# The low part of the queries times the high half of the keys only, with the two maps in the two row halves of the array

## The chip, the core and the metric

The kernel runs on one core of a Trainium2 chip. The core has a matrix engine (TensorE, PE in the rows, with its weight loads as PEld), a vector engine (VectorE, DVE), an activation engine (ScalarE, ACT), a general engine (GpSimd, POOL), and a queue for transfers on SyncE (SP). The metric is the device time of one execution in microseconds (us). Lower is better.

## What is computed

One layer of a backbone with two parallel branches: differential attention and a bidirectional state-space scan. Only the attention over the 2048 latent tokens is touched by the change. Each of 8 heads has two score maps of width 64 and one value of width 128. The keys are the 2048 latent ones and 256 cached ones, 2304 in all.

```python
s = jnp.einsum('bqhcd,bkhcd->bchqk', qi, k).astype(F32) * scale
p = jax.nn.softmax(s, axis=-1)
a = p[:, 0] - lam * p[:, 1]
return jnp.einsum('bhqk,bkhd->bqhd', a.astype(v.dtype), v)
```

Here c is the map (0 or 1). Everything is in float32.

## The kernel before

TensorE takes float32 operands in a fast form (float32r) that rounds them. So the kernel splits every operand into a high part and a low part and adds products of the parts. It runs in three stages: projections and scan (to about 1550 us), attention over the latent tokens (about 1550 to 2790), and the output projection (to the end).

**A unit of attention** is one head and 128 query rows. There are 8 x 16 = 128 units. `frame(i)` writes out the work of four units at different depths: the scores of unit i, the exponentials of unit i-1 (`s_exp`) and its combination of the two maps (`combine`), the transposes of unit i-2 (`t_high`, `t_low`), and the products with the values of the units before that (`av`).

- **Scores.** `s_chunk(i, k)` makes one chunk: map m = k // 3 against 768 keys (j = k % 3). A key tile K (128 x 768) holds the high half of one map's keys in rows 0 to 63 and the low half in rows 64 to 127. The query tile q holds the same part of the queries in both row halves: index l = 0 is the high part, l = 1 the low part. So two matmuls on all 128 rows give (high q) x (high k + low k) and (low q) x (high k + low k). Each is done for two times 384 keys: four matmuls a chunk, 24 a unit. All four write one PSUM tile `ps_s`. The pool `psS` has two of them, for both maps together.
- **Eviction.** One VectorE instruction a chunk copies `ps_s` to the score rows S0 or S1 and takes the row maximum. `s_max` reduces the three maxima of a map to one.
- **Exponentials.** ScalarE makes one exp over 2304 elements for each map, with the row sum (`s_exp`). VectorE turns the two sums into a factor `sm` (reciprocal, then one small instruction), and GpSimd adds the two maps with it (`combine`).
- **Transposes.** Three transposes on TensorE fill one `ps_t`. ScalarE casts it to aH (`t_high`), then VectorE subtracts aH and writes aL (`t_low`): six times a unit.
- **Values.** 54 matmuls into `ps_o` for each pair of units, from aH, aL and V.

**What sets the order.** The code does not issue instructions. It records them in a `Plan`, which gives each a price (`price`) and a due time, plays the program through with these prices, and emits each engine's instructions in the order that comes out. That order is fixed when the kernel is built. Each engine then works strictly in its order, and waits where an operand or a buffer isn't ready.

Every instruction is emitted from one line of the recorder (L232 in the rows), so rows are told apart by the names of the tiles.

Of the kernel before, what the change touches and what calls it, by code (L numbers as in the profile page):

```python
# [9 lines left out]
F32 = mybir.dt.float32  # L10
# [3 lines left out]
ALU = mybir.AluOpType  # L14
# [4 lines left out]
P = 128  # L19
# [7 lines left out]
NKEY = LAT + PAST  # L27
NH = 8
# [166 lines left out]
class Plan:  # L195


    def __init__(self, tc):
        self.tc, self.ops, self.last, self.floor, self.line = tc, [], None, None, None
        for k in ("tensor", "vector", "scalar", "gpsimd", "sync"):  # L200
            setattr(self, k, Engine(self, k))

# [12 lines left out]
    def add(self, eng, name, args, kw):  # L215
        i = len(self.ops)
        if name == "dma_start":
            q, eng = eng, "dma"
        named = dict(kw)
        for k, v in enumerate(args):  # L220
            named["out" if k == 0 else f"arg{k}"] = v
        writes, reads = [], []
        for k, v in named.items():
            if isinstance(v, View):
                (writes if k in ("out", "accum_out") else reads).append(v)
        if name == "matmul" and not kw["start"]:
            reads.append(named["out"])

        def emit():
            rl = lambda v: v.real() if isinstance(v, View) else v  # L230
            e = getattr(self.tc.nc, q if name == "dma_start" else eng)
            getattr(e, name)(*[rl(v) for v in args], **{k: rl(v) for k, v in kw.items()})  # L232

        op = Op(i, eng, emit, self.price(eng, name, named))
        f = str(named.get("func", "")).rsplit(".", 1)[-1]
        op.tab = TABLE.get(f)
        inside = sum(isinstance(v, View) and not v.t.pool.psum and math.prod(v.shape[1:]) > 1
                     for k, v in named.items() if k not in ("out", "accum_out"))
        twice = name in ("tensor_scalar", "tensor_copy") and inside
        op.port = eng == "gpsimd" or eng == "vector" and (inside > 1 or twice)  # L240
        if self.floor is not None:
            op.deps.add(self.floor)
        if self.line is not None and eng == "dma":
            op.weak.update(self.line)
            self.line[:] = [i]
        self.ops.append(op)
        for v in reads + writes:
            s = v.t
            if not s.users:
                op.deps.add(s.pool.op)  # L250
                if s.prev is not None:
                    op.weak.add(s.prev.users[0])
                if s.old is not None:
                    op.deps.update(s.old.users)
                    s.old.dead = True
            else:
                op.weak.add(s.users[0])
            if s.dead:
                raise RuntimeError(f"{s.kw} is used after its slot went to another")
        for v in reads:  # L260
            self.touch(op, v, False)
        for v in writes:
            self.touch(op, v, True)
        op.deps.discard(i)
        op.weak.discard(i)
        op.weak -= op.deps

    def touch(self, op, v, write):
        s = v.t
# [19 lines left out]
    def price(self, eng, name, a):  # L289
        size = lambda v: math.prod(v.shape[1:])  # L290
        o = a.get("out")
        ins = [v for k, v in a.items() if k != "out" and hasattr(v, "shape")]
        if eng == "dma":
            named_in = a["in_"]
            run = min(4096, 4 * min(o.shape[-1], named_in.shape[-1]))
            return max(math.prod(o.shape) * 4 / run * max(9.7 + 0.0365 * run, 28.4) / 16, 180.0) if run > 4 else 180.0
        n = max([size(o)] + [size(v) for v in ins[:1]])
        if eng == "tensor":
            if name == "transpose":
                return 108.0  # L300
            fast = a["lhsT"].t.args[1] == F32R
            m = size(o)
            k = 1.0 if fast else 4.0
            if not fast and a["rhs"].shape[-1] <= 2:
                return 213.0
            return max(m / 2.4 + 13.3, 109.0) if fast else max(m * k / 2.4 + 13.3, 213.0)
        psum = any(isinstance(v, View) and v.t.pool.psum for v in ins)
        if eng == "scalar":
            extra = sum(1 for k in ("bias", "scale") if isinstance(a.get(k), View)) * 93
            return n * 0.833 * 1.0 + (52 if psum else 94) + extra + (93 if "accum_out" in a else 0)  # L310
        if eng == "gpsimd":
            if name == "tensor_tensor":
                thin = any(st[0] == "unsqueeze" and st[1] == (2,) for st in a["in1"].steps)
                return n * (1.66 if thin else 2.1) + 150
            if name == "memset":
                return 36.0
            if name == "tensor_copy":
                return 127.0
            if name == "affine_select":
                return 594.0  # L320
            return n * 0.84 + 240
        if name == "reciprocal":
            return n * 6.25 + 70
        extra = 60 * sum(1 for k in ("scalar", "scalar1", "scalar2") if isinstance(a.get(k), View))
        if name == "tensor_scalar" and not psum:
            return n * 0.53 + 10 + max(extra, 60)
        if name in ("tensor_reduce", "reduce_sum", "reduce_max"):
            return n * (1.042 if ins[0].plain else 1.72) + 70
        return n * 1.042 + 66 + extra
# [113 lines left out]
def body(tc, I, O):  # L443
    pl = Plan(tc)
    nc = pl
    es = ExitStack()
    mm = nc.tensor.matmul
# [254 lines left out]
    for g, wm in enumerate(wms):  # L702
# [4 lines left out]
        if g in (2, 5):  # L707
            for j in range(2):
                acc = vp.tile([P, 384], F32, tag=f"ga{j}", name="macc")[:, :n]
                nc.vector.tensor_scalar(out=acc, in0=wm[:, 0, :n], scalar1=cond[:, j * 8:j * 8 + 1], scalar2=None,  # L710
                                        op0=ALU.mult)
# [8 lines left out]
        ps = bank("y")  # L720
# [4 lines left out]
        for f in range(n // P):  # L725
# [8 lines left out]
                                   op0=ALU.add, op1=ALU.mult)  # L734
# [604 lines left out]
    def load_k(h, m, j):  # L1339
        t = kpool.tile([P, 768], F32R, tag="K", name="K", bufs=9)  # L1340
        for r, src in enumerate((kH_d, kL_d)):
            load(out=t[r * 64:r * 64 + 64].bitcast(F32),
                 in_=src[h, m * 64:m * 64 + 64, SEQ + j * 768:SEQ + (j + 1) * 768])
        Kt[h, m, j] = t
# [127 lines left out]
            u.sm = u.pool.tile([P, 4], F32, tag="sm", name="sm", bufs=2)  # L1472
        return U[i]

    def s_chunk(i, k):
        u = get_unit(i)
        m, j = k // NG, k % NG
        if j == 0:
            u.S[m] = u.pool.tile([P, NKEY], F32, tag=f"S{m}", name=f"S{m}", bufs=2)
        ps = psS.tile([P, 2, 512], F32, tag="S", name="ps_s")  # L1480
        kt = Kt[u.h, m, j]
        for l in range(2):
            for a in range(2):
                mm(ps[:, a, :384], lhsT=u.pr.q[:, l, m, u.qo:u.qo + P], rhs=kt[:, a * 384:(a + 1) * 384],
                   start=l == 0, stop=l == 1)
        src, dst = ps[:, :, :384], u.S[m][:, j * 768:(j + 1) * 768]
        nc.vector.tensor_scalar(out=dst.rearrange("p (a b) -> p a b", a=2), in0=src, scalar1=1.0, scalar2=None,
                                op0=ALU.mult, op1=ALU.max, accum_out=u.mx[:, m, j:j + 1])

    def s_max(i):  # L1490
        u = U[i]
# [91 lines left out]
    def frame(i):  # L1583
        live = i < NU
        if live:
            get_unit(i)
            if i % 2 == 1 and i + 1 < NU:
                get_pair((i + 1) // 2)
        ti = i - 2
        tl = 0 <= ti < NU  # L1590
        if 0 <= i - 1 < NU:
            s_exp(i - 1, 0)
            s_exp(i - 1, 1)
            combine(i - 1)
        j = i - 16
        for k in range(6):
            if live:
                s_chunk(i, k)
                h, r = i // 16, i % 16
                if r == 15 and h + 1 < NH and k >= 3:  # L1600
                    load_k(h + 1, 1, k - 3)
                if r == 5 and h + 1 < NH and k < 3:
                    load_k(h + 1, 0, k)
                if r == 6 and h + 1 < NH and k < 2:
                    load_v(h + 1, k, 0)
            if tl:
                t_high(ti, k)
                t_low(ti, k)
            if k % 2 == 0:
                av((i - 3) * 3 + k // 2 - 1)  # L1610
        if live:
            s_max(i)
        if j >= 0 and j // 16 + 1 < NH:
            if j % 16 == 2:
                load_v(j // 16 + 1, 0, 1)
                load_v(j // 16 + 1, 1, 1)
            if j % 16 == 3:
                load_v(j // 16 + 1, 0, 2)
                load_v(j // 16 + 1, 1, 2)
        U.pop(i - 3, None)  # L1620
# [221 lines left out]
```

## Time and profile before

| what | value |
|---|---|
| median of 3 runs | 3195.61 us (3192.19 to 3200.39) |
| the profiled execution | 3202.35 us, its span 3200.6 us |
| TensorE busy, whole span | 3136.2 us (98%) |
| VectorE, ScalarE, GpSimd busy, whole span | 2321.5, 1907.6, 1302.4 us |
| granted TensorE clock, mean | 0.994 of full speed |

The span reaches from the first to the last instruction; 1.75 us of the profiled time lie around it. Busy shares are means over stages with different limits, so the attention stage has to be read by itself. The ends of matmuls are modelled, so the distance between the starts of neighbouring matmuls tells more than the duration of one.

### The profile page before, as it was taken

The page shows a single profiled execution, that of the slowest core. Times are in us where ns is not written, and L with a number is a line of the kernel's source. Part 1 is how long each engine was busy: PE and PEld are TensorE (multiplying, and loading weights), DVE is VectorE, ACT ScalarE, POOL GpSimd, SP SyncE. Part 2 cuts the span into 40 slices and gives each one's busy share as a digit, 9 for nine tenths or more (in the row PEclk, how much of TensorE's full clock was granted, in tenths as well). Part 3 has the DMA queues.
Part 4 walks back from the last instruction along what each step waited for, and adds up shares of the span by engine and source line. Part 5 has one row for each costly group of instructions (what it writes and reads, how often), then busy time and mean ns, then how long its engine had stood idle before and what let it go on. Part 6 is the DMA issues. An engine that isn't in the chain of part 4 may idle for free. (4 is left out here: it accounts for less than half of the span.)

```text
span 3200.6 us, 55106 instructions
## 1 busy us (share of the span) xinstructions
PE 3136.2 (98%) x19875; PEld 2932.6 (92%) x19875; DVE 2321.5 (73%) x4701; ACT 1907.6 (60%) x3461; POOL 1302.4 (41%) x1120
## 2 busy tenths in 40 slices
PE   8999999999999999999999999999999999999999
PEld 5999999988899999998999999999999999977877
DVE  5544524766665776654599999999999999977775
ACT  4233322333466677663578878888888788864442
POOL 1011000000021122120399999999999999900000
PEclk9999999999999999999999999999999999999999
DMA  8632422867678777878413131313222211296663
GB/s 282 216 113 98 134 81 93 252 185 224 201 224 248 210 212 211 216 188 210 114 34 95 34 97 37 93 40 89 59 75 64 64 51 54 76 282 191 176 189 102
DMA packets 490722, 449.21 MB, mean 140 GB/s; under 512 B 34991, under 2 KB 437704, under 8 KB 490450
## 3 DMA queue, kind: packets, MB, share of 16 engines
q1 hardware_dynamic: 488530, 445.52, 47.6%
q8 instruction: 158, 2.59, 0.3%
q14 instruction: 114, 0.93, 0.1%
q10 hardware_dynamic: 1920, 0.17, 0.0%
HBM read 305.96 MB, written 139.62 MB: 139 GB/s over the span
## 5 line engine op out<-in xcount | busy, mean ns | idle before, releaser
L232 DVE TENSOR_SCALAR_CACHE_REDUCE S<-ps_s 128x768 f32<-128x768 f32 x768 | 716.8, 951 | 17.3 <-PE ps_s L232 11.3
L232 POOL TENSOR_TENSOR S<-S,S 128x768 f32<-128x768 f32 x384 | 710.0, 1866 | 10.1
L232 PE MATMUL ps_p<-hH,wH 128*128 128x384 f32 (+1 forms) x2112 | 698.6, 331 | 0.0
L232 PE MATMUL ps_p<-hL,wH 128*128 128x384 f32 (+1 forms) x2112 | 692.3, 328 | 0.0
L232 PE MATMUL ps_p<-hH,wL 128*128 128x384 f32 (+1 forms) x2112 | 690.9, 327 | 0.0
L232 PE MATMUL ps_s<-K,q 128*128 128x384 f32 x3072 | 678.1, 345 | 0.2
L232 ACT ACTIVATE S<-S,mx 128x2304 f32<-128x2304 f32 x256 | 569.2, 2224 | 82.3 <-DVE mx L232 82.2
L232 PEld LDWEIGHTS ps_s<-K,q 128*128 128x128 f32 x3072 | 504.5, 189 | 3.4 <-DVE S L232 1.1
L232 PE MATMUL ps_o<-aH,V 128*128 128x256 f32 x2304 | 506.4, 295 | 0.1
L232 POOL TENSOR_SCALAR_AFFINE_SELECT ar<-ar 128x512 f32<-128x512 f32 x136 | 115.7, 857 | 786.4 <-ACT ea L232 646.8
L232 DVE TENSOR_TENSOR aL<-ps_t,aH 128x384 fp32r<-128x384 f32 x768 | 406.5, 552 | 40.2 <-ACT aH L232 31.7
L232 ACT CAST aH<-ps_t 128x384 fp32r<-128x384 f32 x768 | 344.3, 478 | 122.2 <-PE ps_t L232 120.7
L232 PEld LDWEIGHTS ps_p<-hL,wH 128*128 128x128 f32 x2112 | 399.3, 189 | 1.7 <-issue 1.4
L232 PEld LDWEIGHTS ps_p<-hH,wH 128*128 128x128 f32 x2112 | 399.4, 189 | 0.9 <-issue 0.5
L232 PEld LDWEIGHTS ps_p<-hH,wL 128*128 128x128 f32 x2112 | 398.8, 189 | 1.3 <-issue 1.2
L232 POOL TENSOR_SCALAR S<-S,sm 128x768 f32<-128x768 f32 x384 | 349.3, 919 | 99.7 <-DVE sm L232 45.5
L232 PEld LDWEIGHTS ps_o<-aH,V 128*128 128x128 f32 x2304 | 382.0, 189 | 0.7 <-ACT aH L232 0.5
L232 PE MATMUL ps_t<-cst,S 128*128 128x128 f32 x2304 | 380.1, 275 | 0.2
L232 PEld LDWEIGHTS ps_t<-cst,S 128*128 128x128 f32 x2304 | 285.4, 140 | 50.4 <-POOL S L232 16.2
L232 PE MATMUL ps_o<-aL,V 128*128 128x256 f32 x1152 | 330.0, 286 | 0.0
L232 DVE TENSOR_TENSOR wL<-wr,wH 128x1024 fp32r<-128x1024 f32 x88 | 108.7, 1235 | 199.6 <-ACT wH L232 196.9
L232 PEld LDWEIGHTS ps_o<-aL,V 128*128 128x128 f32 x1152 | 218.8, 190 | 0.1
(245 smaller groups left out, 4882.1 us busy)
## 6 DMA issues: line engine op xcount, KB each, us to landing
wr<-in_w_in SPq DMA_DIRECT2D x88, 512.0 KB
ar<-row_d SPq DMA_DIRECT2D x68, 512.0 KB
q<-qH_d SPq DMA_DIRECT2D x128, 128.0 KB
q<-qL_d SPq DMA_DIRECT2D x128, 128.0 KB
xb<-xbc_d SPq DMA_DIRECT2D x17, 640.0 KB
K<-kH_d SPq DMA_DIRECT2D x48, 192.0 KB
K<-kL_d SPq DMA_DIRECT2D x48, 192.0 KB
V<-vH_d SPq DMA_DIRECT2D x24, 384.0 KB
```

Of the source, the lines that this page charges most:

```text
L232: getattr(e, name)(*[rl(v) for v in args], **{k: rl(v) for k, v in kw.items()})
```

## The change

The scores of a unit are now made in three pairs (`s_pair`): for the same 768 keys both maps at once, each in its own `ps_s`. The high part of the queries still multiplies both halves of the keys, on all 128 rows. The low part multiplies the high half of the keys only: the product of the two low parts is left out of the sum. That matmul needs 64 rows. The key tile of map 1 is loaded with its halves exchanged (`r ^ m`), so that the high half lies in rows 0 to 63 for map 0 and in rows 64 to 127 for map 1. The four low matmuls of a pair alternate between the two row halves of the array, and `together` makes them one entry of the plan, so that nothing comes between them. The price of a matmul on 64 rows is set anew. The loads of the next head's map 1 are recorded after each pair of a head's last unit, not after the chunks 3 to 5.

```diff
@@ add
+        if self.one:
+            op = self.ops[self.one[0]]
+            op.emit = lambda a=op.emit: (a(), emit())
+            op.cost += self.price(eng, name, named)
+            i = op.i
...
+    def together(self, f):
+
+        self.one = []
+        f()
+        self.one = None
...
@@ price
+            if fast and a["lhsT"].shape[0] == 64:
+                return max(m / 4.8 + 13.3, 109.0)
...
@@ load_k
         for r, src in enumerate((kH_d, kL_d)):
+            r = r ^ m
...
-    def s_chunk(i, k):
+    def s_pair(i, j):
+
         u = get_unit(i)
-        m, j = k // NG, k % NG
         if j == 0:
-            u.S[m] = u.pool.tile([P, NKEY], F32, tag=f"S{m}", name=f"S{m}", bufs=2)
-        ps = psS.tile([P, 2, 512], F32, tag="S", name="ps_s")
-        kt = Kt[u.h, m, j]
-        for l in range(2):
+            for m in range(2):
+                u.S[m] = u.pool.tile([P, NKEY], F32, tag=f"S{m}", name=f"S{m}", bufs=2)
+        ps = [psS.tile([P, 2, 512], F32, tag="S", name="ps_s") for m in range(2)]
+        for m in range(2):
             for a in range(2):
-                mm(ps[:, a, :384], lhsT=u.pr.q[:, l, m, u.qo:u.qo + P], rhs=kt[:, a * 384:(a + 1) * 384],
-                   start=l == 0, stop=l == 1)
...
+                mm(ps[m][:, a, :384], lhsT=u.pr.q[:, 0, m, u.qo:u.qo + P], rhs=Kt[u.h, m, j][:, a * 384:(a + 1) * 384],
+                   start=True, stop=False)
+
+        def low():
+            for a in range(2):
+                for m in range(2):
+                    r = slice(m * 64, m * 64 + 64)
+                    mm(ps[m][:, a, :384], lhsT=u.pr.q[r, 1, m, u.qo:u.qo + P],
+                       rhs=Kt[u.h, m, j][r, a * 384:(a + 1) * 384], start=False, stop=True)
+        pl.together(low)
+        for m in range(2):
+            nc.vector.tensor_scalar(out=u.S[m][:, j * 768:(j + 1) * 768].rearrange("p (a b) -> p a b", a=2),
+                                    in0=ps[m][:, :, :384], scalar1=1.0, scalar2=None,
+                                    op0=ALU.mult, op1=ALU.max, accum_out=u.mx[:, m, j:j + 1])
...
@@ frame
-                s_chunk(i, k)
                 h, r = i // 16, i % 16
-                if r == 15 and h + 1 < NH and k >= 3:
-                    load_k(h + 1, 1, k - 3)
+                if k % 2 == 0:
+                    s_pair(i, k // 2)
+                    if r == 15 and h + 1 < NH:
+                        load_k(h + 1, 1, k // 2)
```

**The order on TensorE, one pair.** These rows of the program before stand in the middle of the attention stage; `ps_s_22446` and `ps_s_22463` are two chunks of the same map, one after the other in the two buffers.

```order
L232 MATMUL ps_s_22446<-K_19977,q_22143 128x384 x4
L232 MATMUL ps_t_22455<-cst_83,S0_22168 128x128 x3
L232 MATMUL ps_s_22463<-K_20048,q_22143 128x384 x4
L232 MATMUL ps_t_22470<-cst_83,S0_22168 128x128 x3
L232 MATMUL ps_o_22339<-aH_22260,V_20261 128x256
```

After the change, one pair is `ps_s_22195` (map 0) and `ps_s_22206` (map 1), the second pair of its unit.

```order
L232 MATMUL ps_s_22195<-K_20050,q_21841 128x384 x2
L232 MATMUL ps_o_22067<-aH_21971,V_20293 128x256
L232 MATMUL ps_o_22067<-aH_21971,V_20286 128x256
L232 MATMUL ps_o_22067<-aL_21983,V_20286 128x256
L232 MATMUL ps_t_22203<-cst_83,S0_21899 128x128
L232 MATMUL ps_s_22206<-K_22071,q_21841 128x384 x2
L232 MATMUL ps_s_22195<-K_20050,q_21841 128x384
L232 MATMUL ps_s_22206<-K_22071,q_21841 128x384
L232 MATMUL ps_s_22195<-K_20050,q_21841 128x384
L232 MATMUL ps_s_22206<-K_22071,q_21841 128x384
L232 MATMUL ps_t_22203<-cst_83,S0_21899 128x128 x2
```

A tile was complete after four matmuls in a row; now both tiles are open until the last of the four low matmuls, and the next pair needs both buffers back.

**The order on VectorE, from the end of one unit into the next.** Before: the last eviction of map 1 of a unit (S1), the first three of map 0 of the next unit (S0), and what lies between. TENSOR_SCALAR from `ps_s` is an eviction, TENSOR_TENSOR aL is `t_low`, TENSOR_REDUCE mx is `s_max`; RECIPROCAL sm and TENSOR_SCALAR sm make the factor for GpSimd.

```order
L232 TENSOR_SCALAR S1_22507,mx_22437<-ps_s_22535 128x768
L232 TENSOR_SCALAR S0_22564,mx_22565<-ps_s_22551 128x768
L232 TENSOR_TENSOR aL_22576<-ps_t_22544,aH_22555 128x3x128
L232 TENSOR_TENSOR aL_22457<-ps_t_22559,aH_22432 128x3x128
L232 TENSOR_REDUCE mx_22437<-mx_22437 128x1
L232 TENSOR_SCALAR S0_22564,mx_22565<-ps_s_22579 128x768
L232 TENSOR_SCALAR S0_22564,mx_22565<-ps_s_22602 128x768
L232 TENSOR_REDUCE mx_22565<-mx_22565 128x1
L232 RECIPROCAL sm_22600<-sm_22600 128x1
L232 TENSOR_SCALAR sm_22600<-l1c_15524,nlam_1341,sm_22600 128x1
L232 TENSOR_TENSOR aL_22497<-ps_t_22593,aH_22485 128x3x128
L232 TENSOR_SCALAR S1_22645,mx_22565<-ps_s_22626 128x768
```

After: the third pair of a unit, its two `s_max`, the first pair of the next unit and the start of its second pair.

```order
L232 TENSOR_SCALAR S0_22034,mx_22035<-ps_s_22088 128x768
L232 TENSOR_SCALAR S1_22045,mx_22035<-ps_s_22095 128x768
L232 TENSOR_TENSOR aL_22015<-ps_t_22106,aH_21989 128x3x128
L232 TENSOR_TENSOR aL_22020<-ps_t_22131,aH_21997 128x3x128
L232 TENSOR_REDUCE mx_22035<-mx_22035 128x1 x2
L232 TENSOR_SCALAR S0_22173,mx_22174<-ps_s_22144 128x768
L232 TENSOR_SCALAR S1_22189,mx_22174<-ps_s_22155 128x768
L232 RECIPROCAL sm_22168<-sm_22168 128x1
L232 TENSOR_TENSOR aL_22218<-ps_t_22178,aH_22208 128x3x128
L232 TENSOR_SCALAR S0_22173,mx_22174<-ps_s_22195 128x768
L232 TENSOR_SCALAR S1_22189,mx_22174<-ps_s_22206 128x768
L232 TENSOR_TENSOR aL_22242<-ps_t_22182,aH_22216 128x3x128
```

The maxima of the two maps were half a unit apart; now both stand behind the unit's last eviction. From here a unit goes on with the small sm instruction, two aL, two evictions, two aL and two maxima, and 118 of the 128 units have this order. ScalarE's order in a unit is the same before and after: exp of map 1, two casts aH, exp of map 0, four casts. The first of those casts belongs to the aL that now stands ahead of the second pair's evictions (here aH_22208, for aL_22218).

**The order on TensorE, the fullest stretch.** After the change, the work between a unit's third pair and the low block of the next unit's first pair, in every second unit. Three transposes and eight `ps_o` matmuls stand directly ahead of these rows; x2 are the high matmuls of map 0, x6 those of map 1 and the four low ones.

```order
L232 MATMUL ps_q<-sqs,one_r 1x256
L232 MATMUL ps_t<-cst,S_26302 128x128 x3
L232 MATMUL ps_o<-aH,V 128x256
L232 MATMUL ps_o<-aL,V 128x256
L232 MATMUL ps_o<-aH,V 128x256
L232 MATMUL ps_s<-K,q 128x384 x2
L232 MATMUL ps_o<-aH,V 128x256
L232 MATMUL ps_o<-aL,V 128x256
L232 MATMUL ps_o<-aH,V 128x256 x2
L232 MATMUL ps_o<-aL,V 128x256
L232 MATMUL ps_s<-K,q 128x384 x6
```

In all, this stretch holds 16 `ps_o` matmuls; the other five of two units hold 0, 10, 9, 11 and 8. Before, nine stood after every second chunk.

## Rows read from the trace of the kernel before

**Rows 1.** Windows: us; busy (instructions) of PE, PEld, DVE, ACT, POOL; clock, DMA.

```profile
1700.00:2200.00 500.00, 500.00 (x3633) 478.38 (x3632) 467.02 (x1149) 405.10 (x652) 464.88 (x366) 1.00 0.26 72
sum 1000.00, PE 1000.00 PEld 956.84 DVE 933.79 ACT 810.34 POOL 929.13; mean PE 500.00 PEld 478.42 DVE 466.90 ACT 405.17 POOL 464.57
```

**Rows 2.** Instructions on tile ps_s, 1700 to 2700: count, ns min/median/max.

```profile
L232 PE MATMUL ps_s<-K,q x2508: 331/336/428, 1699.9 to 2699.1; 128*128 128x384 f32 x193
```

**Rows 3.** Chain of waits, 1700 to 2700: total us, times, longest.

```profile
ACT S L232 <- DVE mx L232: 62.9, 52, 1.2
DVE aL L232 <- ACT aH L232: 25.7, 58, 0.5
```

**Rows 4.** Timeline of PE: start, length of the group, form, count.

```profile
2200.63 0.49 PE L232 MATMUL ps_t<-cst,S 128*128 128x128 f32 x3
...
2202.58 0.40 PE L232 MATMUL ps_o<-aH,V 128*128 128x256 f32 x2
2202.82 0.28 PE L232 MATMUL ps_o<-aL,V 128*128 128x256 f32 x1
...
2203.05 0.28 PE L232 MATMUL ps_q<-sqs,one_r 128*1 128x256 f32 x1
2203.17 1.55 PE L232 MATMUL ps_s<-K,q 128*128 128x384 f32 x8
```

**Rows 5.** Timeline of DVE around a unit's end.

```profile
2022.54 0.95 DVE L232 TENSOR_SCALAR_CACHE_REDUCE S<-ps_s 128x768 f32<-128x768 f32 x1
...
2023.42 0.96 DVE L232 TENSOR_SCALAR_CACHE_REDUCE S<-ps_s 128x768 f32<-128x768 f32 x1
...
2028.20 0.27 DVE L232 TENSOR_SCALAR sm<-l1c,nlam,sm 128x1 f32<-128x1 f32 x1
2028.50 0.56 DVE L232 TENSOR_TENSOR aL<-ps_t,aH 128x384 fp32r<-128x384 f32 x1
...
2029.85 0.55 DVE L232 TENSOR_TENSOR aL<-ps_t,aH 128x384 fp32r<-128x384 f32 x1
2030.32 0.95 DVE L232 TENSOR_SCALAR_CACHE_REDUCE S<-ps_s 128x768 f32<-128x768 f32 x1
```

**Rows 6.** Timeline: an exp that waits for the maximum; an exp and the cast behind it.

```profile
2207.19 0.15 DVE L232 TENSOR_REDUCE mx<-mx 128x1 f32<-128x3 f32 x1
2207.37 2.23 ACT L232 ACTIVATE S<-S,mx 128x2304 f32<-128x2304 f32 x1 [1.21 <-DVE mx L232]
...
2027.99 0.48 ACT L232 CAST aH<-ps_t 128x384 fp32r<-128x384 f32 x1
...
2029.04 2.22 ACT L232 ACTIVATE S<-S,mx 128x2304 f32<-128x2304 f32 x1
...
2031.25 0.84 ACT L232 CAST aH<-ps_t 128x384 fp32r<-128x384 f32 x2
```

**Rows 7.** Timeline: scores that wait for an eviction, then an eviction that waits for scores.

```profile
1578.66 0.96 DVE L232 TENSOR_SCALAR_CACHE_REDUCE S<-ps_s 128x768 f32<-128x768 f32 x1
1579.68 0.65 PEld L232 LDWEIGHTS ps_s<-K,q 128*128 128x128 f32 x4 [0.27 <-DVE S L232]
1579.68 0.98 PE L232 MATMUL ps_s<-K,q 128*128 128x384 f32 x4
...
1567.00 0.86 PE L232 MATMUL ps_s<-K,q 128*128 128x384 f32 x4
1567.90 0.96 DVE L232 TENSOR_SCALAR_CACHE_REDUCE S<-ps_s 128x768 f32<-128x768 f32 x1 [0.18 <-PE ps_s L232]
```

**Rows 8.** Timeline of PE early in the program: matmuls on few rows between full ones.

```profile
16.90 0.49 PE L232 MATMUL ps_y<-wm,cond 128*2 128x384 f32 x1
17.32 0.35 PE L232 MATMUL ps_cb<-cst,mrow 2*128 2x2 f32 x3
17.59 1.45 PE L232 MATMUL ps_y<-wm,cond 128*2 128x384 f32 x4
```

**Rows 9.** DMA: GB/s moved in 40 equal slices of the span.

```profile
GB/s 282 216 113 98 134 81 93 252 185 224 201 224 248 210 212 211 216 188 210 114 34 95 34 97 37 93 40 89 59 75 64 64 51 54 76 282 191 176 189 102
```

More of the change, by code (lines that the diff above doesn't have):

```diff
@@ L198, in __init__ @@
     def __init__(self, tc):
-        self.tc, self.ops, self.last, self.floor, self.line = tc, [], None, None, None
+        self.tc, self.ops, self.last, self.floor, self.line, self.one = tc, [], None, None, None, None
         for k in ("tensor", "vector", "scalar", "gpsimd", "sync"):
@@ L232, in emit @@
             getattr(e, name)(*[rl(v) for v in args], **{k: rl(v) for k, v in kw.items()})
-        op = Op(i, eng, emit, self.price(eng, name, named))
+        if self.one:
[3 more added lines that the diff above has]
+            i = op.i
+        else:
+            op = Op(i, eng, emit, self.price(eng, name, named))
+            self.ops.append(op)
+        if self.one is not None:
+            self.one[:] = [i]
         f = str(named.get("func", "")).rsplit(".", 1)[-1]
@@ L245, in add @@
             self.line[:] = [i]
-        self.ops.append(op)
         for v in reads + writes:
@@ L1473, in get_unit @@
         return U[i]
-    def s_chunk(i, k):
+    def s_pair(i, j):
         u = get_unit(i)
-        m, j = k // NG, k % NG
         if j == 0:
-            u.S[m] = u.pool.tile([P, NKEY], F32, tag=f"S{m}", name=f"S{m}", bufs=2)
-        ps = psS.tile([P, 2, 512], F32, tag="S", name="ps_s")
-        kt = Kt[u.h, m, j]
-        for l in range(2):
+            for m in range(2):
+                u.S[m] = u.pool.tile([P, NKEY], F32, tag=f"S{m}", name=f"S{m}", bufs=2)
+        ps = [psS.tile([P, 2, 512], F32, tag="S", name="ps_s") for m in range(2)]
+        for m in range(2):
             for a in range(2):
-                mm(ps[:, a, :384], lhsT=u.pr.q[:, l, m, u.qo:u.qo + P], rhs=kt[:, a * 384:(a + 1) * 384],
-                   start=l == 0, stop=l == 1)
-        src, dst = ps[:, :, :384], u.S[m][:, j * 768:(j + 1) * 768]
-        nc.vector.tensor_scalar(out=dst.rearrange("p (a b) -> p a b", a=2), in0=src, scalar1=1.0, scalar2=None,
-                                op0=ALU.mult, op1=ALU.max, accum_out=u.mx[:, m, j:j + 1])
+                mm(ps[m][:, a, :384], lhsT=u.pr.q[:, 0, m, u.qo:u.qo + P], rhs=Kt[u.h, m, j][:, a * 384:(a + 1) * 384],
[11 more added lines that the diff above has]
+                                    op0=ALU.mult, op1=ALU.max, accum_out=u.mx[:, m, j:j + 1])
     def s_max(i):
```

## Prediction

> **What bounds the kernel now.** First the windows of the attention stage, the only one touched. In 1000 us of it PE is busy for all 1000, VectorE for 934, GpSimd for 929, ScalarE for 810, at a granted clock of 1.00, the 2.4 GHz level [rows 1]. Busy PE proves little, since matmuls overlap, so I count work by distances between starts. The same 1000 us hold 2508 score matmuls [rows 2]; 24 make a unit, so these are 104.5 units of 9.57 us. Eight scores take 1.55 us; without the last one's 0.336 that is 0.173 each. Transposes, three in 0.49, come 0.108 apart; products with the values 0.12 [rows 2, 4]. A unit is 24 x 0.173 + 18 x 0.108 + 27 x 0.12 + 0.06 (half a ps_q) = 9.39 us. So PE works 9.39 of 9.57 us and sets the pace. VectorE has 934 / 104.5 = 8.94 us of work a unit, GpSimd 8.89. Last, the chain of waits: ScalarE's exp waits for the maxima, 62.9 us in 52 waits, VectorE's aL for the casts, 25.7 us in 58 [rows 3]. No transfer is among them. The reader should see that a relieved PE meets two other engines 0.6 us further down.
>
> **The change, part by part.**
>
> *Low matmuls.* A pair had eight matmuls on 128 rows, 1.38 us. Four remain; the other four go to 64 rows. No row shows two matmuls in two row halves. From below: two at a time and loads hidden, 2 x 0.173 = 0.35 us for four. From above: one after the other as now, 0.69, and more if the array has to empty at each switch. In between: transposes move 128 columns 0.108 apart, which I read as the distance of two weight loads, and each low matmul has its own load: 4 x 0.108 = 0.43. I take 0.43. PE would save 0.26 us a pair; 384 pairs make 100 us.
>
> *Switching the array.* Early in the program three matmuls on two rows stand between full ones. The first starts 0.42 us after the matmul ahead, whose like are 0.32 apart (four in 1.45, the last 0.49), so entering costs 0.10; the three with the way out take 0.27 [rows 8]. A ps_q with one stationary column is followed after 0.12 by the next score, with no gap [rows 4]. I take 0, as at the switch that is nearest in place and data type, and keep 0.10 for the range. The Trainium skill says otherwise (TensorEngine Tiling (Array Packing), Key Properties): a change of tiling mode drains TensorE. By it the change would lose; that is a rival below.
>
> *The two buffers.* Both `ps_s` now fill together and come free one after the other. Count from the start of a pair's first eviction. Evictions follow each other by 0.88 and last 0.95 [rows 5]: both are done at 1.83. Scores that waited for an eviction began 0.06 after it, and four then took 0.98, not 0.86 [rows 7]: 0.18 together. Then the two high matmuls of map 1, 0.35; the low four, the last of which starts 0.32 after the first; and from a last start to the eviction 1567.90 - (1567.00 + 0.86 - 0.336) = 0.37 [rows 2, 7]. So a pair can't follow the pair ahead by less than 1.83 + 0.18 + 0.35 + 0.32 + 0.37 = 3.05 us. Three pairs a unit: 9.15. Before, a chunk had another chunk's whole time to come free.
>
> *VectorE's order.* Behind a first pair's two evictions stands an aL; it needs the first cast, and ScalarE has exp of map 1 ahead of that cast, which needs the maximum. Both maxima now come after the unit's last eviction. So there is a ring: aL, two evictions, aL, small sm, two aL, two evictions, two aL, two maxima (six aL at 0.47, four evictions at 0.88, sm 0.30, maxima 0.27 from two of 0.15: 6.91 us [rows 5, 6]), then exp 0.03 later, 2.22 until the cast can start, cast 0.48, and 0.03 to the next aL [rows 5, 6]. Sum 9.67 us a unit. In the order before, the same ring holds five aL, four evictions and one maximum: 2.35 + 3.52 + 0.15 + 2.76 = 8.78, hidden behind PE's 9.57. So the new order alone lets no unit be shorter than 9.67, whatever the low matmuls cost.
>
> *Both together.* One unit is three distances between first evictions. First to second pair: the ring leaves 3.15 (9.67 - 3.47 - 3.05). Second to third: VectorE's own two evictions 1.76, three aL 1.41 and sm 0.30, 3.47. Third to first: 3.05, the buffers. That is 9.67. In every second unit PE is full in the last of them: its low block ends 1.83 + 0.18 + 0.35 + 0.43 = 2.79 after the second pair's eviction, and six transposes, 16 products, ps_q, four high and four low matmuls follow, 0.65 + 1.92 + 0.12 + 0.69 + 0.43 = 3.81, then 0.26 to the eviction (0.37, less the 0.11 from the last start to the block's end): 6.86 from the second pair on, where the two distances alone make 6.52. That unit is 3.15 + 6.86 = 10.01. Its neighbour starts late enough for the ring to have slack and takes 3.05 + 3.47 + 3.05 = 9.57. Mean 9.79 us, 0.22 more than now, times about 125 units in this steady state (1200 us / 9.57): **+27 us**. Against the profiled execution's 3202 that is 3229; it lies 7 above the median of the runs, so I predict 3196 + 27 = **3223**.
>
> *At nothing.* GpSimd keeps its work; at 8.89 of 9.79 us it has slack. The new order of key loads: six of 192 KB (64 x 768 x 4 bytes) must land within one unit, 120 GB/s; single slices of this span moved 282 [rows 9]. They now stand one behind another on SP, and two value loads that stood between them follow. If that cover were gone, PE would wait at seven head changes, for one key tile of 384 KB each, 2 us at the 200 GB/s of earlier slices. The exchanged halves move the same bytes. Projections, scan and output keep their order.
>
> **The rivals.**
>
> *The halves overlap fully.* Low block 0.35, its last start 0.17 in: the buffers' distance is 2.90, under the 2.97 of VectorE's own work there, and only the ring is left: 9.67, +12, **3208**. For it speaks nothing in the rows but that they don't exclude it. The Trainium skill states it (TensorE: Matmul & The Clock Gate, Part 3): matmuls in different row groups start some 4 ns apart. No run here shows it.
>
> *Serial, or with emptying.* Matmuls one after the other, 0.69, the last start 0.52 in: distances of 3.25, the full unit 3.25 + (3.05 + 4.07 + 0.20), the neighbour 3.25 + 3.47 + 3.25, mean 10.27: +88, **3284**. Emptying instead: 0.20 at each switch (0.37 from a last start to the eviction, less the 0.17 that its columns take): distances of 3.25 again, the full unit 3.25 + (3.19 + 4.21 + 0.06), mean 10.34: +96, **3292**. The second is what the rule of the Trainium skill (TensorEngine Tiling (Array Packing), Key Properties) would do here. Against both stand the small gaps at the switches above, and against the first that nothing makes one row half wait for the other.
>
> *Faster.* The mechanism is PE's relief itself, if VectorE's aL doesn't wait behind the exp. Then PE works 9.39 - 0.78 = 8.61 and VectorE is next with 8.94; with the 0.18 that PE loses today, 9.12 us: -0.45 x 125 = -56, **3140**. It decides where the ring is under 9.5 us: if casts come 0.2 us earlier than I read, or ScalarE is free to start an exp during the last evictions. Against it: both maxima stand behind the last eviction, and VectorE keeps its order.
>
> *The gap at each switch*, 0.10, belongs to the forecast: distances 3.15, the full unit 10.21, its neighbour 9.77, mean 9.99: +52, 3248.
>
> **How the numbers follow.** Forecast with or without the gap 0.47 (its own range 3210 to 3255), full overlap 0.20, serial or emptying 0.20, faster 0.13. About 0.3% (10 us) is what a measurement of this kernel can tell from no change. Faster by more: nearly all of the last case, 0.12. Within: half of the full overlap and a little of the forecast, 0.14. Slower: 0.74. The range leaves out most of the faster case and the top of the serial one: 3180 to 3295.
>
> **What would show it.** In the profile after: 384 x 4 score matmuls on 64 rows. Right: units of 9.7 to 9.9 us; VectorE idle before aL for a cast, about 0.3 us a unit, and before evictions for `ps_s`; PE idle before scores for VectorE; VectorE and GpSimd less busy in 1000 us than before. The starts of the low four decide their price: 0.108 apart, or two at once, or 0.173. A gap ahead of the first low matmul, or of the first full one behind, is the switch. Wrong: if units come under 9.5 us, the ring was misread, and the waits of aL will be short. If they pass 10.1, the low block costs more than 0.53 us.

## The result and the profile after

The changed kernel takes **3267.67 us** (median of 4 runs, 3266.80 to 3270.68) against 3197.02 of the kernel before on the same chip: a ratio of 1.0224, 95% interval 1.0206 to 1.0242, so +71 us. The profiled execution has a span of 3268.9 us at a granted clock of 0.994.

The loss lies in the attention stage. The first two rows are the evictions of `ps_s` over the whole program, of the kernel before and of the changed one: count, ns min/median/max, first and last start.

```profile
L232 DVE TENSOR_SCALAR_CACHE_REDUCE S<-ps_s x768: 935/950/960, 1552.9 to 2779.1; 128x768 f32<-128x768 f32 x192
```

```profile
L232 DVE TENSOR_SCALAR_CACHE_REDUCE S<-ps_s x768: 943/953/960, 1554.5 to 2841.6; 128x768 f32<-128x768 f32 x192
```

From the first eviction to the last it takes 1226.2 us before and 1287.1 after: 61 of the 68 us between the two spans. The other 7 (1.6 ahead of the stage, 5.8 behind) I did not follow up. Below I compare kernels by this length, "the stage".

Next the windows and the instructions on `ps_s` of the changed kernel, for the same 1000 us as [rows 1, 2].

```profile
1700.00:2200.00 500.00, 491.45 (x3465) 395.10 (x3464) 438.49 (x1097) 391.25 (x623) 440.84 (x350) 1.00 0.23 64
sum 1000.00, PE 982.92 PEld 790.42 DVE 876.83 ACT 782.52 POOL 881.56; mean PE 491.46 PEld 395.21 DVE 438.41 ACT 391.26 POOL 440.78
```

```profile
L232 PE MATMUL ps_s<-K,q x2398: 327/338/449, 1700.2 to 2700.0; 128*128 128x384 f32 x100, 64*128 64x384 f32 x100
L232 DVE TENSOR_SCALAR_CACHE_REDUCE S<-ps_s x598: 945/953/959, 1701.3 to 2698.1; 128x768 f32<-128x768 f32 x200
```

24 score matmuls still make a unit, so 2398 are 99.9 units of 10.01 us, where 9.57 stood and 9.79 was forecast. VectorE, GpSimd and ScalarE are all less busy than in [rows 1]: nobody took over as the bound by its own work. The clock is 1.00 in both. So PE, or something that PE waits for, got slower. The chain of waits of the same 1000 us (a list of who waited for whom, as in [rows 3]: us, times, longest) has two new kinds of row for TensorE:

```profile
DVE S L232 <- PE ps_s L232: 86.6, 150, 0.8
...
PEld ps_s L232 <- issue: 74.3, 300, 0.3
ACT S L232 <- DVE mx L232: 57.7, 90, 1.0
PEld ps_s L232 <- DVE S L232: 40.2, 100, 0.6
...
DVE aL L232 <- ACT aH L232: 26.4, 100, 0.3
...
PE ps_s L232 <- DVE S L232: 17.1, 50, 0.3
```

First, TensorE waits for evictions. Its weight loader does so for 40.2 us, 0.40 us a unit. The 17.1 us of PE are no addition: all 50 of these waits stand at a matmul whose load waits too, as here, where the loader's 0.58 holds PE's 0.34:

```profile
2213.62 0.62 PE L232 MATMUL ps_s<-K,q 128*128 128x384 f32 x2 [0.34 <-DVE S L232]
```

```profile
2213.62 0.30 PEld L232 LDWEIGHTS ps_s<-K,q 128*128 128x128 f32 x2 [0.58 <-DVE S L232]
```

The list for the kernel before has neither row in this stretch. That is the turn-around of the two buffers, as forecast. Second, 300 loads for `ps_s`, one for each of the 300 low blocks, stand 0.25 us "for issue": nothing that the profile shows releases them. That is the switch. Its anatomy, in the timeline of one block (start, length of the group, count; the six matmuls are two high ones and the low four):

```profile
2201.70 1.07 PE L232 MATMUL ps_s<-K,q 128*128 128x384 f32 x6
2202.70 0.51 PE L232 MATMUL ps_o<-aH,V 128*128 128x256 f32 x2
```

```profile
2201.88 0.71 PE L232 MATMUL ps_s<-K,q 128*128 128x384 f32 x3
```

```profile
2202.15 0.62 PE L232 MATMUL ps_s<-K,q 64*128 64x384 f32 x4
```

```profile
2202.43 0.34 PE L232 MATMUL ps_s<-K,q 64*128 64x384 f32 x2
```

```profile
2201.59 0.30 PEld L232 LDWEIGHTS ps_s<-K,q 128*128 128x128 f32 x2
2202.15 0.30 PEld L232 LDWEIGHTS ps_s<-K,q 64*128 64x128 f32 x4 [0.25 <-issue]
2202.70 0.30 PEld L232 LDWEIGHTS ps_o<-aH,V 128*128 128x128 f32 x2 [0.25 <-issue]
```

The last three fences of matmuls are narrow windows of the same timeline, which give the single starts. The second high matmul starts at 2201.88. The low four start as two pairs, at 2202.15 and 2202.43; in the trace's own nanoseconds the two of a pair are 3 apart, the median over the 300 blocks. So the row halves do run side by side. But the first pair starts 0.27 behind the last high matmul, not 0.17, and its weight load starts only then, instead of under the matmul ahead. The second pair comes 0.28 later: a load of 0.11 that nothing hides, and 0.17 of columns. The next full matmul comes 0.27 behind that, again with its load unhidden, so that its follower is 0.23 behind it (two in 0.51, the last 0.28) and not 0.12. Sum: 2202.70 - 2201.88 = 0.82; take off the high matmul's own 0.17 and add the 0.11 of delay that is passed on, and the low block costs **0.75** (from unrounded starts). Where a transpose follows, as behind two blocks in three, the delay passed on is half of that and the block costs 0.70. Four full matmuls cost 0.69. The change gives PE nothing back.

### The profile page after: what moved, and what is told of

It is laid out like the page before. It is cut to its first block, busy times and chain, and to the rows that moved or that the text cites. A ratio compares the mean times of both kernels' runs of the same rounds, so it can differ in the third digit from the quotient of the medians.

```text
span 3268.9 us, 54904 instructions
## 1 busy us (share of the span) xinstructions
PE 3175.3 (97%) x19875; PEld 2775.9 (85%) x19875; DVE 2305.1 (71%) x4701; ACT 1919.0 (59%) x3461; POOL 1293.6 (40%) x1120
## 4 chain that ended last, share of the span: by engine, by line
PE 77%; DMA 10%; DVE 8%; ACT 2%; issue 2%; SPq 1%; POOL 0%; DVEq 0%; ACTq 0%; POOLq 0%
PE ps_p L232 27%; PE ps_s L232 16%; PE ps_o L232 13%; PE ps_t L232 7%; PE ps_y L232 5%; PE ps_v L232 5%; PE ps_f L232 3%; DVE S L232 2%; DMA ya<-y_d 1%; DMA yz<-z_d 1%; DMA hb<-hb_d 1%; SPq L232 1%; DMA rb<-rs_d 1%; DVE ya L232 1%; PE ps_tr L232 1%
## 5 line engine op out<-in xcount | busy, mean ns | idle before, releaser
L232 DVE TENSOR_SCALAR_CACHE_REDUCE S<-ps_s 128x768 f32<-128x768 f32 x768 | 703.6, 953 | 126.9 <-PE ps_s L232 122.7
L232 PE MATMUL ps_s<-K,q 128*128 128x384 f32 (+1 forms) x3072 | 632.4, 374 | 25.5 <-DVE S L232 25.3
L232 PE MATMUL ps_o<-aH,V 128*128 128x256 f32 x2304 | 516.6, 296 | 0.0
L232 PEld LDWEIGHTS ps_s<-K,q 128*128 128x128 f32 (+1 forms) x3072 | 348.1, 187 | 161.4 <-issue 95.1
L232 PE MATMUL ps_o<-aL,V 128*128 128x256 f32 x1152 | 341.7, 297 | 0.3 <-DVE aL L232 0.3
L232 PEld LDWEIGHTS ps_t<-cst,S 128*128 128x128 f32 x2304 | 258.0, 141 | 82.3 <-issue 48.8
```

## The experiments

Theory 1: the two row halves overlap, but the switch in and out costs what that saves, so PE is not relieved; the rest of the loss is the pair form, in which both buffers fill and come free together. Theory 2: the switch alone is the loss and the pair form is harmless. Ratios are to the kernel before, measured on the same chip; "stage" is defined above (1226 before, 1287 changed).

**The pair form without a switch.** The low four go to all 128 rows and keep the price and the order of the changed kernel; they multiply the low part of the queries with both halves of the keys again.

```diff
-            if fast and a["lhsT"].shape[0] == 64:
+            if fast and self.one is not None:
...
-                    r = slice(m * 64, m * 64 + 64)
-                    mm(ps[m][:, a, :384], lhsT=u.pr.q[r, 1, m, u.qo:u.qo + P],
-                       rhs=Kt[u.h, m, j][r, a * 384:(a + 1) * 384], start=False, stop=True)
+                    mm(ps[m][:, a, :384], lhsT=u.pr.q[:, 1, m, u.qo:u.qo + P],
+                       rhs=Kt[u.h, m, j][:, a * 384:(a + 1) * 384], start=False, stop=True)
```

> The pair form of the changed kernel with the same order on every engine, but the four low matmuls run on all 128 rows again (so the product of the two low parts is back in the sum): no switch of the array. Theory 1 (the pair form costs by itself, and the low block is one price in it): four matmuls one after the other, last start 0.52 us into the block, distance of two pairs 1.83 + 0.18 + 0.35 + 0.52 + 0.37 = 3.25 us, units of 10.2 to 10.3 us, 3280 to 3290 us in all, no faster than the changed kernel. Theory 2 (the switches of the array alone are the loss, the pair form is harmless): units near the 9.6 us of before, 3195 to 3215 us.

Measured: 3257.57, ratio 1.0197 (1.0182 to 1.0212), +63 us; stage 1280.9. With no switch at all nine tenths of the loss are there: theory 2 falls. The chain of waits for 1700 to 2700 of this kernel shows where, and behind it its score matmuls in that time:

```profile
DVE S L232 <- PE ps_s L232: 77.2, 150, 0.7
...
ACT S L232 <- DVE mx L232: 53.7, 52, 1.1
PEld ps_s L232 <- DVE S L232: 37.5, 100, 0.6
...
PE ps_s L232 <- DVE S L232: 15.9, 50, 0.3
...
PEld ps_t L232 <- POOL S L232: 12.7, 50, 0.3
```

```profile
L232 PE MATMUL ps_s<-K,q x2408: 331/337/446, 1699.9 to 2699.8; 128*128 128x384 f32 x186
```

TensorE's loader waits 37.5 us for evictions, 0.37 us a unit, with PE's 15.9 inside them, and the 300 waits for issue are gone. A unit takes 9.97 us, 0.40 more than before, so the waits have nearly the size of the loss. The expected 3280 to 3290 was too high since I let the eviction of map 0 wait for all four low matmuls; it needs the third.

**What one more step in the same block costs.** The low four are done twice within one switch, at half the price each so that the order stays.

```diff
-                return max(m / 4.8 + 13.3, 109.0)
+                return max(m / 4.8 + 13.3, 109.0) / 2
...
-            for a in range(2):
-                for m in range(2):
+            for n, a, m in [(n, a, m) for n in range(2) for a in range(2) for m in range(2)]:
...
```

> The changed kernel with the four low matmuls written twice in one block (the low product counts double), price halved so that the order stays. Theory 1 (a switch costs about 0.20 us each way, inside a block the halves overlap and loads are hidden): four more matmuls add 2 x 0.173 = 0.35 us a pair, units of about 11.05 us, 3395 us. Rival (each low matmul costs its weight load of 0.108): 0.43 more a pair, about 3430 us. Rival (each four low matmuls cost what the first four do, 0.75): about 3550 us.

Measured: 3393.55, ratio 1.0623 (1.0605 to 1.0641), +126 over the changed kernel: 0.33 us for two more steps, 0.16 a step that does two matmuls. Four matmuls without a new switch thus cost 0.33, the lower bound that the prediction named; the rest of the 0.70 to 0.75, some 0.4, is the switch.

**Twice as many switches, same work.** One high matmul is moved into the middle of the low block.

```diff
-        for m in range(2):
-            for a in range(2):
-                mm(ps[m][:, a, :384], lhsT=u.pr.q[:, 0, m, u.qo:u.qo + P], rhs=Kt[u.h, m, j][:, a * 384:(a + 1) * 384],
-                   start=True, stop=False)
+        def high(m, a):
...
+        for m, a in ((0, 0), (0, 1), (1, 0)):
+            high(m, a)
...
             for a in range(2):
+                if a:
+                    high(1, 1)
```

> The changed kernel with the low block cut in two by one full-row matmul that it had anyway (the second high one of map 1): same work, twice as many switches. Theory 1 (0.094 us of emptying and 0.108 of an exposed weight load at each switch): 0.40 us more a pair, about 1.2 a unit, 3410 to 3425 us. As the prediction had it (a switch costs nothing): unchanged, 3268 us.

Measured: 3412.49, ratio 1.0678 (1.0662 to 1.0694), +145 over the changed kernel: 0.38 us for each of 384 more switches in and out.

**One, then three, single matmuls on 64 rows in the kernel before**, order unchanged; those matmuls leave half of their terms out.

```diff
-                mm(ps[:, a, :384], lhsT=u.pr.q[:, l, m, u.qo:u.qo + P], rhs=kt[:, a * 384:(a + 1) * 384],
+                r = slice(0, 64 if k % 2 == 0 and l == 1 and a == 0 else P)
+                mm(ps[:, a, :384], lhsT=u.pr.q[r, l, m, u.qo:u.qo + P], rhs=kt[r, a * 384:(a + 1) * 384],
```

(That is the one with three; the other has it once a unit.)

> The kernel before with one of a unit's 24 score matmuls on 64 rows (low queries times high keys, for 384 keys of one chunk; the low-low product is left out there): 128 entries and 128 exits, nothing else changed, order the same. Theory 1 (0.20 us each way): 0.40 us a unit on the engine that sets the pace, up to 51 us: 3235 to 3250 us. If the switch is free: 3197 us.

> The kernel before with three of the 24 score matmuls of a unit on 64 rows, each alone between full ones (one in every second chunk), where one64 had one; the low part of their product loses half its terms. If a switch in and out costs 0.40 us and one64's 0.24 was that less the slack of PE in a unit, 0.24 + 2 x 0.40 = 1.04 us a unit times 128 is +133: 3320 to 3335. If each costs 0.24, +93: 3285 to 3295. If one64's loss had to do with its place alone, under 3250.

Measured: 3225.89, ratio 1.0096 (1.0081 to 1.0111), and 3325.61, ratio 1.0406 (1.0391 to 1.0422): +31 and +129. The step from one to three is 98 us in 128 units, 0.38 us for each switch in and out. The first costs 0.24; the unit's slack of 0.18 would make up the difference. The timeline of the loads in the kernel with one shows both ends of it:

```profile
2203.12 0.30 PEld L232 LDWEIGHTS ps_s<-K,q 128*128 128x128 f32 x2
2203.67 0.18 PEld L232 LDWEIGHTS ps_s<-K,q 64*128 64x128 f32 x1 [0.25 <-issue]
2204.04 0.19 PEld L232 LDWEIGHTS ps_s<-K,q 128*128 128x128 f32 x1 [0.18 <-issue]
```

The lone matmul's load starts 0.25 after PE's loader went idle, and the next full one's 0.18 after; behind a lone step the way out takes 0.37 (2204.04 - 2203.67), behind two steps 0.27. The 0.37 is the 0.28 that lies between the two steps of a block and the gap of 0.09 again, so it need not be a cost of its own.

**The switch in the chunks of before.** Each chunk keeps its own buffer and its place in the order; its two low matmuls go to the two row halves, and the key tiles are loaded to suit (not shown).

```diff
-                mm(ps[:, a, :384], lhsT=u.pr.q[:, l, m, u.qo:u.qo + P], rhs=kt[:, a * 384:(a + 1) * 384],
+                r = slice(a * 64, a * 64 + 64) if l else slice(0, P)
+                mm(ps[:, a, :384], lhsT=u.pr.q[r, l, m, u.qo:u.qo + P], rhs=kt[r, a * 384:(a + 1) * 384],
```

> The kernel before in its own chunks and practically its own order (a chunk is one map and 768 keys, its two high matmuls on 128 rows), but with the chunk's two low matmuls in the two row halves, one for each 384 keys; the key tiles are laid out for it. No pair of maps, no shared buffers, no late maximum: only the switch, twice as many as in the changed kernel, with one low step each where that has two. With the changed kernel's distances (0.27 in, 0.27 out, one load of 0.11 unhidden, two steps fewer) a chunk costs PE 0.12 us more than four full matmuls, 0.71 a unit; less the 0.18 of slack in 9.57 that is 0.53 to 0.71 a unit, times 128: 3265 to 3290. If the switch were free, PE would be relieved of 1.04 us a unit and the kernel would come to 3140 to 3195.

Measured: 3314.69, ratio 1.0371 (1.0356 to 1.0387), +118, 25 over the top of what I expected: I had taken the way out behind two steps, 0.27, for blocks of one step, and the rows above show 0.37 there. The chain of waits for 1700 to 2700 has the switches and no wait of PE for an eviction:

```profile
PEld ps_s L232 <- issue: 142.0, 572, 0.3
DVE S L232 <- PE ps_s L232: 95.4, 334, 0.5
...
PEld ps_t L232 <- issue: 88.2, 476, 0.2
```

So the switch and the pair form are two losses that can be had one without the other.

**Does the order within the block matter?** Both halves of map 0's keys ahead of map 1's.

```diff
-            for a in range(2):
-                for m in range(2):
+            for m in range(2):
+                for a in range(2):
```

> The changed kernel with its low four in another order, both halves of map 0's keys ahead of both of map 1's, all else at its place. If the two row halves overlap only where neighbours lie in different halves, the four now start at 0, about 0.17 to 0.28, 3 ns behind that, and again 0.17 to 0.28 on: the block has three steps where it had two, costs 0.17 to 0.28 us more, and the kernel takes 65 to 105 us more than the changed one, 3333 to 3373. If the array runs the halves free of each other whatever the order, or the weight loads alone set the pace, it stays within 10 us of 3268.

Measured: 3266.33, ratio 1.0219 (1.0202 to 1.0236), as the changed kernel. Its block has the same two steps:

```profile
2201.49 0.30 PEld L232 LDWEIGHTS ps_s<-K,q 64*128 64x128 f32 x4 [0.25 <-issue]
2202.05 0.31 PEld L232 LDWEIGHTS ps_t<-cst,S 128*128 128x128 f32 x3 [0.25 <-issue]
```

From the first low load to the first full one it takes 0.56, as 0.55 above. The half to which a record belongs is not in the trace, so how the four are matched I can't show; only that neighbours need not lie in different halves.

**Is it the order under a wrong price?** The first kernel is the pair form on all rows as above, but planned with the price that full matmuls have; the second is the changed kernel, planned with 0.19 us for a matmul on 64 rows (the lines below).

```diff
-                return max(m / 4.8 + 13.3, 109.0)
+                return 188.0
```

> The pair form with the four low matmuls on all 128 rows, as in pair_full, but planned with the price of four full matmuls, so that the order of the whole program may differ. Theory 1 (the pair form itself costs: both ps_s fill together and come free together, and both maxima come last) expects it to stay at 3245 to 3270, near pair_full's 3258. The rival, that the order was planned with too small a price and that this is the loss, expects 3195 to 3215.

> The changed kernel as it is, but planned with 0.19 us for a matmul on 64 rows, 0.75 for the block of four, which is what the trace of it shows; the order of the whole program may differ. Theory 1 expects 3250 to 3275, since the block takes the same time in whatever order, and the two buffers come free as before. The rival (the order under the wrong price is the loss) expects 3195 to 3220.

Measured: 3287.50, ratio 1.0290 (1.0274 to 1.0305), and 3301.76, ratio 1.0331 (1.0315 to 1.0346). They are 30 and 34 us slower than with the small price, and over the top of both expectations. So the price was not the loss; but the order does count, and the honest price makes the worse one. The chain of waits for 1700 to 2700 of the first shows a part of it:

```profile
PEld ps_t L232 <- POOL S L232: 35.3, 98, 0.5
...
PEld ps_s L232 <- DVE S L232: 17.7, 74, 0.3
```

The wait for evictions is half of the 37.5 us above, but the transposes now wait 35.3 us for GpSimd's combination, where 12.7 stood. Why the planner's order comes to that, I didn't follow.

**Is it the late maxima?** Once alone, in the kernel before, with one reduction for both maps; once undone in the pair form, with pairs of chunks that follow each other in the old order, so that map 0 is complete in mid-unit; that with and without the switch.

```diff
-        for m in range(2):
-            nc.vector.tensor_reduce(out=u.mx[:, m, 3:4], in_=u.mx[:, m, 0:NG], axis=AX.X, op=ALU.max, negate=True)
+        nc.vector.tensor_reduce(out=u.mx[:, :, 3:4], in_=u.mx[:, :, 0:NG], axis=AX.X, op=ALU.max, negate=True)
```

```diff
-            r = r ^ m
+            r = r ^ (m * NG + j) % 2
...
+        both = [(k // NG, k % NG) for k in (2 * j, 2 * j + 1)]
...
```

> The kernel before, with one reduction for both maps' maxima, so that both exps wait for the last eviction of a unit, as they do after the change; no other part of the change. It tests the ring by itself: the prediction's 9.67 us a unit against 9.57 gives +12 us, 3205 to 3210. If the ring was misread, or the maxima's place is harmless, it stays within 5 us of 3195. If a late maximum is the larger part of what the pair form costs, it comes to 3230 or more.

> The changed kernel with other pairs: a pair is two chunks that follow each other in the order before (map 0 keys 0 and 1; map 0 keys 2 with map 1 keys 0; map 1 keys 1 and 2), so that map 0's scores and its maximum are ready in the middle of a unit, as before the change. Low block, switches and the two buffers that fill and come free together stay. If the late maxima (the ring) are what the pair form costs, it takes 3200 to 3225, the rest being the low block's 0.75 against 0.69. If the buffers are, it stays at 3255 to 3270.

> The same pairs of chunks as in seq_pair, with the four low matmuls on all 128 rows, planned as if they had the low price: no switch at all. If the late maxima are what the pair form costs, 3195 to 3205, as before. If the buffers that come free together are, 3245 to 3260, as in pair_full.

Measured: one reduction 3237.54, ratio 1.0128 (1.0113 to 1.0143), +40; the other pairs with the switch 3261.04, 1.0203 (1.0188 to 1.0218), and without it 3253.68, 1.0179 (1.0162 to 1.0196). Undoing the late maxima brings the pair form 4 to 7 us. What stays is the wait for the buffers; the chain of waits for 1700 to 2700 of the pairs without a switch:

```profile
DVE S L232 <- PE ps_s L232: 81.7, 150, 1.0
...
PEld ps_s L232 <- DVE S L232: 54.1, 135, 0.9
ACT S L232 <- DVE mx L232: 38.2, 33, 1.6
...
PE ps_s L232 <- DVE S L232: 21.9, 51, 0.7
```

The loader waits 54.1 us for evictions, against 37.5 with late maxima, while exps wait less for the maximum (38.2 us, against 53.7). So a part of what the earlier maxima gave may have been lost again at the buffers; the 4 to 7 us are what undoing them brought, not shown to be all that they cost. The single reduction lies above the 3230 at which I would have called the late maxima the larger part, but it is no clean test: the planner made another order from it, so its +40 is the late maxima together with that order.

## Why the prediction was right and wrong

The direction was right and the size was not: +71 against +27. The step that failed is *Low matmuls*, "I take 0.43", together with *Switching the array*, "I take 0". The block costs 0.70 to 0.75.

*Low matmuls.* Both ends were misplaced. Below, 0.35 is right for the work without a switch, as two more steps cost 0.33, but no block comes without one. Above, 0.69 was called the serial price; the block costs that with full overlap, since the switch comes on top. My in-between of four loads 0.108 apart is nothing that happens: loads come in pairs too, 0.30 for four.

*Switching.* I leaned on the one-column `ps_q`, which stands between scores without a gap [rows 4], and on rows 8 as an upper bound of 0.10. A matmul with 64 active rows is not like a `ps_q`, which reads all 128. The 0.10 of [rows 8] was the right size of a gap (0.09 here); I kept it for the range alone, and did not count the loads that the switch leaves unhidden. The trace of the kernel before shows one at the place of [rows 8]:

```profile
16.13 0.55 DVE L232 COPY mrow<-ps_y 2x384 f32<-2x384 f32 x1 [3.91 <-PE ps_y L232]
...
17.31 0.26 PEld L232 LDWEIGHTS ps_cb<-cst,mrow 2*128 2x128 f32 x3 [0.65 <-DVE mrow L232]
```

The first load for two rows starts at 17.31, 0.01 ahead of its own matmul, and not under the matmul ahead. The row puts that down to VectorE, whose copy had ended at 16.68 (16.13 + 0.55), so it was another cause. Two gaps of 0.09 and two loads of 0.11 are 0.40; the experiments gave 0.38 twice (more switches, and one against three lone matmuls) and some 0.4 a third time (the doubled block). The Trainium skill's rule (TensorEngine Tiling (Array Packing), Key Properties: a change of tiling mode drains TensorE) and its rule of overlap (TensorE: Matmul & The Clock Gate, Part 3: starts some 4 ns apart) stood in the prediction as two rivals, each with its own time. The trace agrees with the second by the 3 ns within a pair, and the gap of 0.09 at each switch fits the first. Each alone would have given 3208 or 3292, and the measured time lies between.

*The two buffers and both together.* Right in mechanism and nearly in size. Put the block's middle price of 0.72 into the same walk, with the low starts where they are (0.09 of gap, 0.28 between pairs): distances are 1.83 + 0.18 + 0.35 + 0.37 + 0.37 = 3.10; the full unit is 3.10 + 3.08 + 4.10 + 0.02 = 10.30, its neighbour 3.10 + 3.47 + 3.10 = 9.67, the mean 9.99, +0.42 a unit and +52 us. The variant with a gap of 0.10, kept for the range, had come to the same 9.99 from other parts (0.43 for the four, a gap on either side), so the unit's time alone would not tell the two apart; the starts do.

The walk has one slip. It let a pair's first eviction wait for the last of the four low matmuls, as the note on TensorE's order has it too, but map 0's tile is complete with the third. At the assumed 0.108 from one to the next that made the forecast longer, and without it the miss would have been larger. In the changed kernel third and fourth start together, so nothing hangs on it. For the pair form without a switch the walk, with the third, gives 1.83 + 0.18 + 0.35 + 0.35 + 0.37 = 3.08 between pairs, units of 10.23 and 9.63 and a mean of 9.93, near the 9.97 measured there. The timeline of VectorE in the changed kernel shows the two units (the first eviction of each pair, and two aL that wait for a cast):

```profile
2202.90 0.96 DVE L232 TENSOR_SCALAR_CACHE_REDUCE S<-ps_s 128x768 f32<-128x768 f32 x1 [0.77 <-PE ps_s L232]
...
2206.07 0.96 DVE L232 TENSOR_SCALAR_CACHE_REDUCE S<-ps_s 128x768 f32<-128x768 f32 x1 [0.70 <-PE ps_s L232]
...
2209.41 0.95 DVE L232 TENSOR_SCALAR_CACHE_REDUCE S<-ps_s 128x768 f32<-128x768 f32 x1
...
2212.60 0.96 DVE L232 TENSOR_SCALAR_CACHE_REDUCE S<-ps_s 128x768 f32<-128x768 f32 x1 [0.29 <-PE ps_s L232]
...
2215.12 0.56 DVE L232 TENSOR_TENSOR aL<-ps_t,aH 128x384 fp32r<-128x384 f32 x1 [0.34 <-ACT aH L232]
2215.69 0.96 DVE L232 TENSOR_SCALAR_CACHE_REDUCE S<-ps_s 128x768 f32<-128x768 f32 x1
...
2218.37 1.02 DVE L232 TENSOR_TENSOR aL<-ps_t,aH 128x384 fp32r<-128x384 f32 x2 [0.19 <-ACT aH L232]
2219.31 0.95 DVE L232 TENSOR_SCALAR_CACHE_REDUCE S<-ps_s 128x768 f32<-128x768 f32 x1
...
2222.93 0.96 DVE L232 TENSOR_SCALAR_CACHE_REDUCE S<-ps_s 128x768 f32<-128x768 f32 x1 [0.73 <-PE ps_s L232]
```

The neighbour is 3.17 + 3.34 + 3.19 = 9.70, the full unit 3.09 + 3.62 + 3.62 = 10.33: the walk's alternation, 0.03 above it each. So the mis-sized term carries 25 of the 44 us that were missing (52 for 27). Of the others, 9 are small excesses within the stage (61 measured there), 7 lie outside it, and 2 are the profiled executions against the medians.

*VectorE's order (the ring).* It was said to forbid units under 9.67. The runs don't bear it out as a term of its own: without the late maxima the pair form is only 4 to 7 us faster, though other waits grew there. The waits of aL for casts are in the trace, 26.4 us or 0.26 a unit where about 0.3 was forecast, but both rows above fall into the full unit, where PE waits for no more evictions after 2213.62 and its own work sets the length. That both mechanisms ask for 3.1 and 3.5 between pairs may be why the walk came out all the same.

*At nothing.* GpSimd and the key loads kept their cover: no wait for a key tile stands in the whole list of which rows are shown above.

*The signs named ahead.* "If they pass 10.1, the low block costs more than 0.53" proved too lax a mark: units of 10.01 went with a block of 0.72. The signs of the mechanism came: the waits of aL, VectorE's before evictions (86.6 us), TensorE's for evictions, and less work in 1000 us for VectorE and GpSimd.

Which share of the pair form's +63 is the two buffers rests on the loader's waits for evictions: 0.37 of the 0.40 us by which its units are longer, none before. A kernel that shortens only the evictions, or has a second pair of buffers, was not run, so that share is read from the trace and not shown by a change. The pair form in the order from the honest price is a warning: there this wait is half as long, and the kernel is 30 us slower. So the +63 is shown for the pair form together with the order that the planner made of it.

## What to carry to other kernels

Splitting a matmul into row halves pays only if enough work stands within one switch: here a switch in and out costs 0.38 to 0.40 us, and each step of two matmuls saves 0.17 against two full ones, so by estimate from these numbers a block needs more than two steps of 384 columns to gain anything; no run here gained time by it. Count the switch twice (in and out), each with its gap and its unhidden weight load. And whoever fills two buffers together to make room for such a block must count the turn-around: with two buffers in all, TensorE waited 0.37 to 0.40 us a unit for evictions. The pair form cost 63 us here without any switch, and these waits have nearly that size.

## What the runs showed of the hardware

- Two matmuls on different row halves start 3 ns apart, and a step of two costs 0.16 to 0.17 us for 384 columns, as one full matmul does.
- Entering or leaving a 64-row stretch opens a gap of 0.09 us, and the first weight load behind it (0.11) does not run under the matmul ahead. A lone step has a longer way out, 0.37 against 0.27 behind two steps, which show 0.28 between them.
- The order of the four within the block made no difference (3266.33 against 3267.67).
